# A row-sum kernel whose tile context is closed empty at the start, with all its work behind it on hand-made semaphores

## The chip, the cores and the metric

The kernel runs on one core of one Trainium2 chip. The metric is the device time of one execution in microseconds; the number given for a kernel is the median of its runs. Before the change it is 161.99 us (three runs, 161.81 to 162.04).

## What is computed

```python
def setup_inputs():
    batch, seq, dim = 32, 512, 1024
    return {"x": np.random.randn(batch, seq, dim).astype(np.float32), "multiplier": 0.5}

def reference(x, multiplier):
    return (np.sum(x, axis=-1) * multiplier).astype(np.float32)
```

16,384 rows of 1,024 floats each become one float each. The input is 67.1 MB, the output 64 KB.

## The kernel before

**Tiling.** Each of the 128 partitions owns 128 rows, taken as 8 blocks of 16 rows. A block is one tile `xb` of 128 x 16 x 1024 floats (8.4 MB), and three such buffers are used in turn. The first seven blocks are loaded by one transfer each (L98). The last block comes in five pieces: rows 0 to 7, 8 to 12 and 13 to 14 into the same kind of buffer (L117), and the last row in two parts, 544 and 480 floats, into a small tile `end` (L123). All transfers are issued by SP, on one queue.

**Compute.** VectorE (DVE) sums the 16 rows of a block with one `reduce_sum` into `sums` (L100) and scales them into `res` with a small instruction (L103). In the seventh block DVE takes only 8 rows; ScalarE (ACT) does the other 8, each by one `activation` with an accumulator (L74). ACT needs a table load ahead of its first activation. In the last block both share the rows: ACT the rows in `on_act`, DVE the others, by `tensor_tensor_reduce` (L84). The last row is two such instructions on `end`: `first` when its first part has landed, and `final`, which also folds in the result of `first`.

**Stores.** The results of the first seven blocks leave by an early store (L127, 56 KB), the last block's by the last store (L145, 8 KB). Both stand on SP's queue behind all loads.

**Order and waits.** The tile context works out the waits from the tiles: a load into a buffer waits until the DVE has read what lay in it, an instruction waits for its load, and so on. Where the kernel wants a wait in a place of its own, `nop_after` (L63) puts an empty instruction with that wait on an engine. The context also owns what stands at the end of the program: on its exit (L208 in the profile) SP waits for the last store, all five engines meet at a barrier, GpSimd (POOL) clears the range of semaphores that the context used, and all five meet at a second barrier. The program's entry (L194) has a barrier of the same build. `start_loads_at_entry` takes the leading loads of SP, those that wait for nothing (three, one for each buffer), and puts them ahead of SP's part in the entry barrier, so that the first transfer is SP's first instruction.

Of the kernel before, what the change touches and what calls it, by code (L numbers as in the profile page):

```python
# [1 line left out]

# [4 lines left out]


@with_exitstack
def kernel(  # L10
    ctx: ExitStack,
    tc: tile.TileContext,
    x: bass.AP,
    multiplier: float,
    out: bass.AP,
):

    nc = tc.nc
    P = nc.NUM_PARTITIONS
    fp32 = mybir.dt.float32  # L30
    ADD = mybir.AluOpType.add

    x_flat = x.flatten_outer_dims()
    N, D = x_flat.shape
    rows = N // P
    out_flat = out.rearrange("b s -> (b s)")
    mul = float(multiplier)

    B = 16
    n_blocks = rows // B  # L40
    assert N == P * rows and rows == n_blocks * B
    own = rows - B
    x_rows = x_flat[0 : P * own, :].rearrange("(p c) d -> p c d", p=P)
    x_last = x_flat[P * own : N, :].rearrange("(p c) d -> p c d", p=P)
    out_rows = out_flat[0 : P * own].rearrange("(p c) -> p c", p=P)
    out_last = out_flat[P * own : N].rearrange("(p c) -> p c", p=P)

    x_pool = ctx.enter_context(tc.tile_pool(name="x", bufs=3))
    res_pool = ctx.enter_context(tc.tile_pool(name="res", bufs=1))
    sums = res_pool.tile([P, rows], fp32, name="sums")  # L50
    res = res_pool.tile([P, rows], fp32, name="res")
    cut = 544
    at = 576
    end = res_pool.tile([P, at + D - cut], fp32, name="end")
    nc.vector.memset(end[:, at - 2 : at], 0.0)  # L55

    SYNC = mybir.DependencyInfo(mybir.DependencyClass.Sync, mybir.DependencyReason.DATA)
    ORDER = mybir.DependencyInfo(
        mybir.DependencyClass.NoSync, mybir.DependencyReason.SCHED_ONLY
    )  # L60

    def nop_after(engine, waits_for, follows):
        i = engine.nop()  # L63
        for w in waits_for:
            tc.add_manual_dep(i.ins, w.ins.name, SYNC, reason="end seen here")
        for f in follows:
            tc.add_manual_dep(i.ins, f.ins.name, ORDER, reason="in this order")
        return i

    loads = []  # L70
    acts = []

    def act_row(t, r, col):
        acts.append(nc.scalar.activation(  # L74
            out=t[:, r, :],
            in_=t[:, r, :],
            func=mybir.ActivationFunctionType.Copy,
            scale=mul,
            accum_out=res[:, col : col + 1],
        ))  # L80

    def dve_sum(row, dst, scale):
        mid = row.shape[-1] // 2
        return nc.vector.tensor_tensor_reduce(  # L84
            out=row[:, 0:mid],
            in0=row[:, 0:mid],
            in1=row[:, mid:],
            scale=scale,
            scalar=0.0,
            op0=ADD,  # L90
            op1=ADD,
            accum_out=dst,
        )

    for b in range(n_blocks - 1):
        c0 = b * B
        t = x_pool.tile([P, B, D], fp32, name="xb")
        loads.append(nc.sync.dma_start(out=t, in_=x_rows[:, c0 : c0 + B, :]))  # L98
        h = B if b < n_blocks - 2 else B // 2
        nc.vector.reduce_sum(  # L100
            out=sums[:, c0 : c0 + h], in_=t[:, 0:h, :], axis=mybir.AxisListType.X
        )
        nc.vector.tensor_single_scalar(  # L103
            out=res[:, c0 : c0 + h],
            in_=sums[:, c0 : c0 + h],
            scalar=mul,
            op=mybir.AluOpType.mult,
        )
        for r in range(h, B):
            act_row(t, r, c0 + r)  # L110

    c0 = (n_blocks - 1) * B
    t = x_pool.tile([P, B, D], fp32, name="xb")
    pieces = [(0, 8), (8, 13), (13, 15)]
    for lo, hi in pieces:
        loads.append(
            nc.sync.dma_start(  # L117
                out=t[:, lo:hi, :], in_=x_last[:, lo:hi, :]
            )
        )  # L120
    for to, lo, hi in ((0, 0, cut), (at, cut, D)):
        loads.append(
            nc.sync.dma_start(  # L123
                out=end[:, to : to + hi - lo], in_=x_last[:, B - 1, lo:hi]
            )
        )
    early = nc.sync.dma_start(out=out_rows, in_=res[:, 0:own])  # L127
    on_act = {4, 5, 6, 7, 11, 12, 14}
    for r in range(B - 1):
        if r in on_act:  # L130
            act_row(t, r, c0 + r)
        else:
            dve_sum(t[:, r, :], res[:, c0 + r : c0 + r + 1], mul)
    first = dve_sum(end[:, 0:cut], end[:, at - 1 : at], 1.0)
    part_seen = nop_after(nc.vector, [first], [])
    final = dve_sum(end[:, at - 2 :], res[:, rows - 1 : rows], mul)

    tc.add_manual_dep(final.ins, part_seen.ins.name, ORDER, reason="in this order")
    tc.declare_no_dep(final.ins, first.ins.name, reason="waited for by the nop in front")

    seen = nop_after(nc.sync, loads[-8:] + acts[-1:], [])
    store = nc.sync.dma_start(out=out_last, in_=res[:, own:])  # L145
    tc.add_manual_dep(store.ins, seen.ins.name, ORDER, reason="in this order")
    for a in acts[-len(on_act) :]:
        tc.declare_no_dep(store.ins, a.ins.name, reason="waited for by the nop in front")
    nop_after(nc.sync, [early, final], [store])

    def start_loads_at_entry(nc_):

        entry, *rest = nc_.main_func.blocks
        is_sp = lambda i: i.engine == mybir.EngineType.SP
        is_load = lambda i: type(i).__name__ == "InstDMACopy"
        for block in rest:
            body = list(block.instructions)
            own = [i for i in body if is_sp(i)]  # L160
            if not any(is_load(i) for i in own):
                continue
            lead = []
            for i in own:
                if not is_load(i) or i.sync_info.on_wait:
                    break
                lead.append(i)
            names = {i.name for i in lead}
            block.instructions = [i for i in body if i.name not in names]
            head = list(entry.instructions)  # L170
            at = next(
                k for k, i in enumerate(head) if is_sp(i) and type(i).__name__ == "InstDrain"
            )
            entry.instructions = head[:at] + lead + head[at:]
            return

    nc.at_finalize(start_loads_at_entry)


# [1 line left out]
_INS = ['x', 'multiplier']  # L181
_OUTS = [((32, 512), 'float32')]

_NUMBERS = {'multiplier': 0.5}


# [26 lines left out]
```

## The time and the profile before

| what | value |
|---|---|
| median of three runs | 161.99 us |
| span of the profiled execution, first to last instruction | 160.2 us |
| median less this span (the page gives the profiled execution no time of its own beside the span) | 1.79 us |
| DMA queue: bytes, share of 16 engines' span | 67.18 MB, 97.6% |
| DVE busy | 119.3 us (74%) |
| ACT busy | 17.3 us (11%) |
| POOL busy | 0.2 us |

The span counts from the first to the last instruction on any engine, waits and barriers included; the busy times leave out register, branch, semaphore and DMA-issuing instructions. SP does no arithmetic and shows only as `SPq`: its issues of transfers and its semaphore instructions. A transfer's time from issue to landing includes the time in which it stands behind others in the queue.

### The profile page before, as it was taken

The numbers are of one execution on the slowest core, as the hardware profiler recorded it, in microseconds if no ns is written. First come the engines' busy times: TensorE is split into PE (matmuls) and PEld (weight loads), VectorE is DVE, ScalarE is ACT, GpSimd is POOL, SyncE is SP. The second block draws the span as 40 slices with busy tenths as digits, with TensorE's granted clock in tenths as the row PEclk, the third lists the DMA queues.
The fourth block names the chain that finished last, engine by engine and source line by source line (L and its number), as shares of the span: only waits on it lengthen the run. The fifth ranks groups of instructions, "written<-read, shape, count | busy, mean of one in ns | idle before, by whom it ended". The sixth has DMA issues, their size and how long they took to land.

```text
span 160.2 us, 139 instructions
## 1 busy us (share of the span) xinstructions
DVE 119.3 (74%) x35; ACT 17.3 (11%) x31; POOL 0.2 (0%) x4
## 2 busy tenths in 40 slices
DVE  0000059998799968999599995999959999597543
ACT  0000000000000000000000000000000000599952
POOL 0000000000000000000000000000000000000000
DMA  8996996996996997997998989979969969999992
GB/s 278 507 524 262 524 524 262 524 524 262 524 507 278 524 475 311 524 442 344 524 425 360 524 360 425 524 327 458 524 295 491 524 278 507 393 401 422 424 395 76
DMA packets 2016, 67.18 MB, mean 419 GB/s; under 512 B 480, under 2 KB 608, under 8 KB 736
## 3 DMA queue, kind: packets, MB, share of 16 engines
q1 hardware_dynamic: 2016, 67.18, 97.6%
HBM read 67.11 MB, written 0.07 MB: 419 GB/s over the span
## 4 chain that ended last, share of the span: by engine, by line
DMA 75%; DVE 22%; SPq 1%; issue 0%; DVEq 0%
DMA xb<-in_x_dram 51%; DMA end<-in_x_dram 24%; DVE sums L100 22%; SPq L117 1%; SPq L123 0%; DVE end L84 0%; SPq L98 0%; DVE res L103 0%; DVEq L208 0%
## 5 line engine op out<-in xcount | busy, mean ns | idle before, releaser
L100 DVE TENSOR_REDUCE sums<-xb 128x16 f32<-128x16384 f32 (+1 forms) x7 | 112.0, 16002 | 31.5 <-DMA xb<-in_x_dram 31.5
L74 ACT ACT_TABLE_LOAD x1 | 1.3, 1283 | 138.0 <-DMA xb<-in_x_dram 138.0
L74 ACT ACTIVATE xb<-xb 128x1024 f32<-128x1024 f32 x15 | 15.7, 1044 | 2.1 <-DMA xb<-in_x_dram 2.1
L84 DVE CUSTOM_DVE_ANT_0 xb<-xb 128x512 f32<-128x512 f32 x8 | 5.1, 690 | 4.9 <-DMA xb<-in_x_dram 4.9
L74 ACT ACTIVATION_READ_ACCUMULATOR xb<-xb 128x1 f32 x15 | 2.8, 187 | 0.0
L55 DVE MEMSET end<- 128x2 f32 x1 | 0.1, 60 | 1.8 <-PEq L194 1.8
L103 DVE TENSOR_SCALAR res<-sums 128x16 f32<-128x16 f32 (+1 forms) x7 | 1.2, 174 | 0.2
L84 DVE CUSTOM_DVE_ANT_0 end<-end 128x272 f32<-128x272 f32 (+1 forms) x2 | 0.9, 426 | 0.2 <-DMA end<-in_x_dram 0.2
L84 DVE DVE_READ_ACCUMULATOR2_ANT res<- 128x1 f32 x9 | 0.7, 83 | 0.0
L194 POOL MEMSET const-bfloat16-1.0<- 128x1 bf16 x1 | 0.1, 102 | 0.0
L194 POOL MEMSET const-uint8-127<- 128x1 uint8 x1 | 0.1, 102 | 0.0
L194 POOL MEMSET const-float32-0.0<- 128x1 f32 x1 | 0.1, 99 | 0.2 <-issue 0.2
L194 POOL MEMSET const-float32-1.0<- 128x1 f32 x1 | 0.1, 99 | 0.0
L84 DVE DVE_READ_ACCUMULATOR2_ANT end<- 128x1 f32 x1 | 0.1, 83 | 0.0
## 6 DMA issues: line engine op xcount, KB each, us to landing
xb<-in_x_dram SPq DMA_DIRECT2D x1, 4096.0 KB, 31.1
xb<-in_x_dram SPq DMA_DIRECT2D x1, 2560.0 KB, 36.9
xb<-in_x_dram SPq DMA_DIRECT2D x1, 1024.0 KB, 38.9
end<-in_x_dram SPq DMA_DIRECT2D x1, 272.0 KB, 39.0
end<-in_x_dram SPq DMA_DIRECT2D x1, 240.0 KB, 39.2
xb<-in_x_dram SPq DMA_DIRECT2D x7, 40.8
out_dram<-res SPq DMA_DIRECT2D x1, 56.0 KB, 10.0
out_dram<-res SPq DMA_DIRECT2D x1, 8.0 KB, 1.4
```

Of the source, the lines that this page charges most:

```text
L55: nc.vector.memset(end[:, at - 2 : at], 0.0)
L74: acts.append(nc.scalar.activation(out=t[:, r, :], in_=t[:, r, :], func=mybir.ActivationFunctionType.Copy, scale=mul, accum_out=res[:, col ...
L84: return nc.vector.tensor_tensor_reduce(out=row[:, 0:mid], in0=row[:, 0:mid], in1=row[:, mid:], scale=scale, scalar=0.0, op0=ADD, op1=ADD, ...
L100: nc.vector.reduce_sum(out=sums[:, c0 : c0 + h], in_=t[:, 0:h, :], axis=mybir.AxisListType.X)
L103: nc.vector.tensor_single_scalar(out=res[:, c0 : c0 + h], in_=sums[:, c0 : c0 + h], scalar=mul, op=mybir.AluOpType.mult,)
L117: nc.sync.dma_start(out=t[:, lo:hi, :], in_=x_last[:, lo:hi, :])
L194: nc = _bacc.Bacc("TRN2", target_bir_lowering=False, num_devices=1)
```

## The change

The tile context is closed and compiled as soon as the kernel function starts, with nothing in it. What it puts at its end (two barriers, with no semaphores to clear) therefore stands right behind the program's entry, and a new body of the program begins after it. Everything else is written with plain SBUF tensors and semaphores by hand: one semaphore for each load, one counting DVE's instructions and one counting ACT's. The loads, the arithmetic, the split between the engines, the sizes and `start_loads_at_entry` are as before. At its end SP waits for the two stores, and the program ends there.

```diff
     nc = tc.nc
+    tc.close()
+    tc.compile()
+    nc.switch_body("work")
...
+    def load(name, dst, src, free=None):
+        landed = sem(name)
+        i = nc.sync.dma_start(out=dst, in_=src)
+        if free is not None:
+            i.wait_op(dve_done, free, "sem-ge")
+        i.then_inc(landed, 16)
+        return landed
...
-        loads.append(nc.sync.dma_start(out=t, in_=x_rows[:, c0 : c0 + B, :]))
+        t = buf[b % bufs]
+        landed = load(
+            f"landed{b}",
+            t,
+            x_rows[:, c0 : c0 + B, :],
+            freed[b - bufs] if b >= bufs else None,
+        )
...
+        if h < B:
+            nc.scalar.wait_ge(landed, 16)
+            for r in range(h, B):
+                i = act_row(t, r, c0 + r)
+            early_act = marks(i, "act")
...
+    nc.sync.wait_ge(dve_done, early_dve)
     early = nc.sync.dma_start(out=out_rows, in_=res[:, 0:own])
+    early.wait_op(act_done, early_act, "sem-ge")
...
-    part_seen = nop_after(nc.vector, [first], [])
+    part = marks(first, "dve")
+    nc.vector.wait_ge(dve_done, part)
     final = dve_sum(end[:, at - 2 :], res[:, rows - 1 : rows], mul)
+    final.wait_op(landed_end[1], 16, "sem-ge")
+    done = marks(final, "dve")
...
-    seen = nop_after(nc.sync, loads[-8:] + acts[-1:], [])
+    nc.sync.wait_ge(act_done, late_act)
     store = nc.sync.dma_start(out=out_last, in_=res[:, own:])
-    nop_after(nc.sync, [early, final], [store])
+    store.wait_op(dve_done, done, "sem-ge")
+    stored = sem("stored")
+    store.then_inc(stored, 16)
+    nc.sync.wait_ge(early_stored, 16)
+    nc.sync.wait_ge(stored, 16)
```

In the order of the built program the three leading loads are still SP's first instructions, ahead of the entry barrier. Two things in it are not in the diff's words: the ACT table load now stands directly behind the barriers, with no wait on a load in front of it, and the second and third `xb` buffers have exchanged their addresses.

## The prediction

> **What bounds the kernel now.** I read the page's totals first, then the timeline, then the records of the context's closing line (L208), then SP's own waits. From the page:
>
> ```profile
> span 160.2 us, 139 instructions
> ...
> DVE 119.3 (74%) x35; ACT 17.3 (11%) x31; POOL 0.2 (0%) x4
> ...
> q1 hardware_dynamic: 2016, 67.18, 97.6%
> ```
>
> The DMA queue is busy for 97.6% of the span and DVE for 74%, so the input stream sets the pace. The timeline (start us, duration us, what, and in brackets the idle time before it) shows how closely:
>
> ```profile
> 0.00 97.51 SPq L98 DMA_DIRECT2D xb<-in_x_dram  x7
> ...
> 1.81 0.06 DVE L55 MEMSET end<- 128x2 f32 x1 [1.81 <-PEq L194]
> 21.91 17.22 DVE L100 TENSOR_REDUCE sums<-xb 128x16 f32<-128x16384 f32 x1 [20.04 <-DMA xb<-in_x_dram]
> ...
> 41.23 17.22 DVE L100 TENSOR_REDUCE sums<-xb 128x16 f32<-128x16384 f32 x1 [1.89 <-DMA xb<-in_x_dram]
> ...
> 138.05 1.28 ACT L74 ACT_TABLE_LOAD   x1 [138.05 <-DMA xb<-in_x_dram]
> ...
> 157.58 0.41 DVE L84 CUSTOM_DVE_ANT_0 end<-end 128x241 f32<-128x241 f32 x1 [0.16 <-DMA end<-in_x_dram]
> 157.91 0.08 DVE L84 DVE_READ_ACCUMULATOR2_ANT res<- 128x1 f32 x1
> 158.02 0.34 SPq L145 DMA_DIRECT2D out_dram<-res  x1
> ```
>
> Every reduction starts when its load lands. The last piece of input lands just before 157.58, DVE works 0.41 us on it, the last store is issued at 158.02, and the page's sixth part gives it 1.4 us to landing: 159.4. The span ends at 160.2. The chain of waits stops at DVE's closing drain at 157.99 and so leaves out this tail; it is in the records of L208 (duration least/median/most in ns, then first and last start in us):
>
> ```profile
> L208 POOLq EVENT_SEMAPHORE  x4: 17/17/17, 159.6 to 160.1; - x4
> ...
> L208 SPq DRAIN  x3: 7/7/7, 159.5 to 159.8; - x3
> ...
> L208 PEldq EVENT_SEMAPHORE  x2: 51/51/51, 159.7 to 160.2; - x2
> ...
> L208 POOLq EVENT_SEMAPHORE_RANGE_CLEAR  x1: 93/93/93, 159.8 to 159.8; - x1
> ```
>
> The first SP drain is where the last store is seen; its record starts at 159.468. The last record, TensorE's release from the second barrier, starts at 160.153 and takes 0.051: 160.204. The stretch between is one barrier (released at about 159.7), the clearing of semaphores, and a second barrier: 160.204 - 159.468 = 0.74 us in which nothing of the problem is done and nothing else runs.
>
> **The change part by part, on the profiled execution (span 160.20).** The runs' median lies 1.79 us above this span. The page shows no time of the profiled execution itself, so I carry 1.79 over as a constant; whether it is one is a rival below.
>
> *The tail.* What stands behind the last store's landing goes: 0.74 us. In its place SP has one semaphore instruction that waits for both stores; SP's two-wait instructions ahead of L145 last 0.028 us. The early store has landed by then (issued at 147.79, 10.0 us to landing, 157.8). Net 0.74 - 0.03 = **-0.71 us**. No other engine works there, so all of it is on the path.
>
> *The head.* The two barriers now run behind the entry barrier, which ends at about 1.7 us. At the tail the two rounds took 0.74 us, the clear included, so the engines come free at about 2.4 instead of 1.7. DVE's memset (1.81) moves to about 2.5; its first reduction waits until 21.91, 19 us of cover. SP's first three loads stand ahead of all barriers in the built program's order, so the stream still starts at 0.00. SP's fourth load waits for the first reduction's end at 39.1, 36 us later. Cost 0. If the cover were gone, as it would be were the loads behind the barriers, the whole stream would start about 2.4 us later.
>
> *The ACT table load.* It no longer waits for a load and moves from 138.05 into the idle 2.4 to 21.9. ACT's first activation then starts at about 138.05 instead of 139.34, and its eight rows end at about 146.5 instead of 147.8. What is late next: the first piece of the last block, which lands at 147.7, and the second, whose rows start at 153.79. ACT is caught by these loads again, so nothing reaches the end: 0.
>
> *The early store.* SP holds it for ACT:
>
> ```profile
> SPq L127 <- DVE res L103: 28.0, 1, 28.0
> ...
> SPq L208 <- DMA out_dram<-res: 1.0, 1, 1.0
> ...
> SPq L127 <- ACT xb L74: 0.9, 1, 0.9
> ```
>
> That wait of 0.9 us goes; DVE's scaling at 146.70 + 0.17 is late next, so it is issued at about 146.95 instead of 147.79. All loads were issued by 118.9, and the store stayed behind them (10.0 us to landing) until the last input had landed at 157.55. I take 0. If its packets do get in between, they push the last load back by at most 56 KB at the page's mean 419 GB/s = 0.13 us; an earlier store could instead take up to the same from what stands behind the loads. Bounds -0.13 to +0.13.
>
> *Waits by hand.* Each reduction, activation and load waits for the same event as before. SP loses its second wait ahead of the buffered loads (17 ns each, long over when DVE ends) and four of the waiting instructions ahead of the last store. These end by 157.76, and DVE's last result comes at 157.99, so SP waits there anyhow: 0. DVE keeps its one wait between `first` and `final` (0.021 us at 157.45, before the last part lands at 157.55). Behind SP's new wait for ACT stands only the last store, and ACT's last row ended at 157.44, before DVE's. At most the order of SP's waking changes; from rows of 0.02 to 0.03 us I bound it by -0.03 to +0.03.
>
> *Buffers.* The second and third buffer exchange addresses. In the timeline the reductions start at 21.91, 41.23, 60.58, 79.94, 99.28, 118.63 and 137.98, so spacings are 19.32 to 19.36 whichever buffer is filled and whichever is read. I take 0; both ends are 0.04 us for each of seven loads, -0.28 to +0.28. The value taken is the one nearest to these rows, which show no dependence.
>
> Sum: 160.20 - 0.71 = 159.49 for the span, and 161.99 - 0.71 = **161.28 us** for the time (-0.44%). A measurement of this kernel can tell about 0.2%, 0.32 us, from no change; -0.71 is more than twice that.
>
> **A rule beside the rows.** Nothing in the trace shows the 1.79 us around the span. The Trainium skill, "Runtime: NRT & Kernel Launch", section "The ~15µs preamble/postamble breakdown", says that the runtime puts its own barrier of about 1.5 us behind every kernel and then resets 51 semaphores on each engine in about 1.5 us. That speaks against the change in one way: a meeting of the engines is still paid after the kernel's barriers are gone. But by that rule it was paid before as well, and on a fixed count of semaphores, so the estimate by the page is again -0.71. By its stages of 1.5 + 1.5 + 2 us after the kernel, more than 1.79 us, they cannot all be inside the measured time; no row settles which are.
>
> **The rivals.**
>
> *The outside shrinks too.* TensorE and POOL now end at about 2.4 us and only SP is late at the end. If part of the 1.79 us is work that each engine does for itself after its last instruction, four engines do it under the cover of the kernel. The nearest row is the second barrier with its clear, 159.77 to 160.20 = 0.43 us. That gives 161.28 - 0.43 = 160.85. For it: all five engines end within 0.1 us today. Against it: SP, still last, does its own part uncovered.
>
> *The outside grows by what was cut.* If the measured end is a meeting that takes its full time from when the last engine arrives, and it had been running alongside the kernel's own barriers, the cut of 0.71 is given back: 161.99, no change. For it: nothing in the trace shows the measured end. Against: all engines left the last barrier at 160.15 to 160.20, so such a meeting could hardly begin before.
>
> *The leftover semaphores are cleared elsewhere: slower.* Before, POOL clears the context's ten in one 0.093 us instruction. After, sixteen hand-made ones are left standing. If what follows the kernel clears them one by one, at the 0.078 us between two successive POOL semaphore instructions of the barrier, this costs 16 x 0.078 = 1.25 us after the span: 161.28 + 1.25 = 162.53. It decides from 1.03 us on (0.71 + 0.32), 0.065 us each. At the bare 0.017 us of such an instruction it is 0.27 and the kernel stays faster. Against it: a clear of a range took 0.093.
>
> *The change doesn't do what it says.* If nobody clears them, every wait of a second execution is already met. DVE would run its 119.3 us without waiting and the program would end near 1.8 + 119.3 + 1.8 = 123 us, with sums of what an earlier execution left. The two barriers in the head clear nothing, so this can't be excluded from the trace.
>
> **How the numbers follow.** The forecast, with its small bounds (-0.13, -0.03, -0.28 on one side, the same on the other, partly together: 160.95 to 161.6), has 0.70. The outside shrinking (160.85) 0.12; giving back (161.99) 0.10; cleared one by one (162.53) 0.05; uncleared (123) 0.03. Faster by over 0.2%: 0.70 + 0.12 + 0.03 = 0.85; within: 0.10; slower: 0.05. The range runs from below 160.85, at 160.75, to 161.65, and leaves out 0.18.
>
> **What would show it.** In the changed profile SP's last record waits for the stores and ends near 159.5, with no barrier records behind it. Two barrier rounds stand between 1.7 and 2.5 us. The table load stands there too. The first reduction starts at 21.9, the spacings stay 19.3, the early store is issued near 146.95, and `final` starts near 157.58. I am wrong if the first load no longer starts the span, if the spacings move by 0.1 us, or if the span falls by 0.7 and the runs' time doesn't.

## The result, and the profile after the change

The changed kernel takes **160.73 us** (median of five runs, 160.69 to 160.89); the kernel before took 161.84 beside it (161.79 to 162.04, five runs, three of them those already told). The ratio is 0.9929, 95% interval 0.9917 to 0.9941: about 1.15 us faster. The forecast was 161.28 with a range of 160.75 to 161.65: the sign was right, the gain was under-estimated by 0.4 to 0.5 us, and the time lies 0.02 us under the range.

The page of the changed kernel:

```profile
span 159.4 us, 123 instructions
...
DVE 119.3 (75%) x35; ACT 17.3 (11%) x31; POOL 0.2 (0%) x4
...
q1 hardware_dynamic: 2016, 67.18, 98.0%
```

The work is the same; the span fell from 160.2 to 159.4. The timeline (start us, duration us, what, idle before):

```profile
2.39 1.28 ACT L82 ACT_TABLE_LOAD   x1 [2.39 <-PEq L26]
2.46 0.06 DVE L103 MEMSET end<- 128x2 f32 x1 [2.46 <-PEq L26]
21.84 17.22 DVE L117 TENSOR_REDUCE sums<-xb 128x16 f32<-128x16384 f32 x1 [19.31 <-DMA xb<-in_x_dram]
...
41.18 17.22 DVE L117 TENSOR_REDUCE sums<-xb 128x16 f32<-128x16384 f32 x1 [1.91 <-DMA xb<-in_x_dram]
...
157.51 0.41 DVE L92 CUSTOM_DVE_ANT_0 end<-end 128x241 f32<-128x241 f32 x1 [0.15 <-DMA end<-in_x_dram]
157.85 0.08 DVE L92 DVE_READ_ACCUMULATOR2_ANT res<- 128x1 f32 x1
157.96 0.34 SPq L175 DMA_DIRECT2D out_dram<-res  x1
```

The stream starts and runs as before, within 0.07 us at every reduction and at `final`. The closing barriers are in the head, at the line that compiles the empty context (L26; durations in ns, then first and last start in us), and after the last store only SP's wait is left (L180, a view of its own):

```profile
L26 POOLq EVENT_SEMAPHORE  x4: 17/17/17, 1.9 to 2.3; - x4
...
L26 PEldq EVENT_SEMAPHORE  x2: 51/51/51, 2.0 to 2.3; - x2
```

```profile
L180 SPq EVENT_SEMAPHORE  x1: 28/28/28, 159.4 to 159.4; - x1
```

All of this is as forecast. What was not: the profiled run's own time is 160.73, so the time above the span is 160.73 - 159.42 = 1.31 us. In the runs of before beside the experiments, time less span (given to 0.1 us) is 1.73 to 1.83 in each. The constant of 1.79 is no constant; it lost 0.48 us, and that is the part of the gain that the sum lacked.

### The profile page after: what moved, and what is told of

Read it like the earlier page. It is cut to its first block, busy times and chain, and to the rows that moved or that the text cites. A ratio compares the mean times of both kernels' runs of the same rounds, so it can differ in the third digit from the quotient of the medians.

```text
span 159.4 us, 123 instructions
## 1 busy us (share of the span) xinstructions
DVE 119.3 (75%) x35; ACT 17.3 (11%) x31; POOL 0.2 (0%) x4
## 4 chain that ended last, share of the span: by engine, by line
DMA 76%; DVE 22%; SPq 1%; issue 0%
DMA xb<-in_x_dram 51%; DMA end<-in_x_dram 25%; DVE sums L117 22%; SPq L75 1%; DVE end L92 0%; DVE res L123 0%; DVE res L92 0%
## 6 DMA issues: line engine op xcount, KB each, us to landing
out_dram<-res SPq DMA_DIRECT2D x1, 56.0 KB, 10.8
```

## The experiments

**Theory 1**: something of each engine's own follows its last instruction inside the measured time (its "own end" below), the engines do it side by side, and the time is the latest of last record + own end. The change leaves four engines' ends under the cover of the kernel. **Theory 2**: the time around the span became shorter for another reason, such as fewer branches, a shorter program or the missing clear. Each experiment was run beside runs of the kernel before, and its ratio is to those; the time above the span is taken run by run, and the median is given. A record is one instruction in the profile; its views round starts to 0.1 us, and the ends given to 0.01 us below are read from the same records.

The kernel before took 161.93 to 161.99 us (medians) beside the experiments, and 161.84 beside the result. So differences of medians between two experiments are good to about 0.1 us only, and several medians lie 0.01 to 0.07 us above the range that was written down for their outcome: all engines (161.28) and GpSimd alone (161.32, both for at most 161.25), the barrier of four (161.42 for 161.39), the head alone (162.02 for 161.99), the left semaphores and the late table (160.81 and 160.83 for 160.80).

### All engines wait for the last store

```diff
     nc.sync.wait_ge(early_stored, 16)
     nc.sync.wait_ge(stored, 16)
+    nc.tensor.wait_ge(stored, 16)
+    nc.gpsimd.wait_ge(stored, 16)
+    nc.scalar.wait_ge(stored, 16)
+    nc.vector.wait_ge(stored, 16)
```

> The changed kernel with four waits added: TensorE, GpSimd, ScalarE and VectorE also wait for the last store, so all five engines end together, with no barrier. The span can grow by 0.05 us at most (one semaphore instruction of 0.02 to 0.05 us side by side on each). Theory 1 (each engine has something of its own to do after its last instruction, inside the measured time; the change lets four engines do it under cover): the time above the span returns from 1.31 to 1.64-1.79 us, so the time is 161.05 to 161.25. Theory 2 (the time around the span became shorter for another reason: fewer branches, fewer instructions, no clear of semaphores at the end): the time above the span stays 1.31, the time is 160.73 to 160.80.

Measured: 161.28 us (161.23 to 161.31), ratio 0.9957 (0.9944 to 0.9971). The last record of each engine, each from the view of its own line:

```profile
L180 SPq EVENT_SEMAPHORE  x1: 28/28/28, 159.4 to 159.4; - x1
...
L181 PEldq EVENT_SEMAPHORE  x1: 51/51/51, 159.4 to 159.4; - x1
...
L182 POOLq EVENT_SEMAPHORE  x1: 17/17/17, 159.4 to 159.4; - x1
...
L183 ACTq EVENT_SEMAPHORE  x1: 17/17/17, 159.4 to 159.4; - x1
...
L184 DVEq EVENT_SEMAPHORE  x1: 21/21/21, 159.4 to 159.4; - x1
```

All five engines end between 159.43 and 159.47, with a span of 159.5, and the time above it is 1.81 us, near that of the kernel before. There is no barrier, no clear, no branch more than in the changed kernel. Theory 2 falls: which engines end late decides, and that alone gives back 0.45 us of the gain by the ratios, 0.55 by the medians.

### One engine at a time

The same edit with the TensorE line alone:

```diff
+    nc.tensor.wait_ge(stored, 16)
```

> The changed kernel with one wait added: TensorE alone also waits for the last store. Theory 1, with TensorE the engine whose end costs most: 161.05 to 161.25, as with all engines; theory 1 with another engine the costly one: 160.73 to 160.80. Theory 2: 160.73 to 160.80.

Measured: 161.10 us (161.02 to 161.24), ratio 0.9947 (0.9935 to 0.996). And with the GpSimd line alone:

```diff
+    nc.gpsimd.wait_ge(stored, 16)
```

> The changed kernel with one wait added: GpSimd alone also waits for the last store. Theory 1, with GpSimd the engine whose end costs most: 161.05 to 161.25; with another engine the costly one: 160.73 to 160.80. Theory 2: 160.73 to 160.80.

Measured: 161.32 us (161.24 to 161.52), ratio 0.9961 (0.9948 to 0.9973): as much as all four together, so the ends do not add up; the longest counts. TensorE's time lies in the range written down for the engine whose end costs most, but that range was set too low: TensorE's end costs too, but less than GpSimd's. The profiled run of the GpSimd kernel took 161.52, with this one added record (its L181):

```profile
L181 POOLq EVENT_SEMAPHORE  x1: 17/17/17, 159.7 to 159.7; - x1
```

It ends with SP's last record (159.67 and 159.68), and yet this run's time lies 161.52 - 159.67 = 1.85 above it instead of 1.31. With the same 1.85, GpSimd's end at 159.44 in the run of all engines gives 161.29; that run took 161.28.

### GpSimd waits, but ends sooner

```diff
+    nc.gpsimd.wait_ge(dve_done, done)
```

> The changed kernel with one wait added: GpSimd also waits, but for VectorE's last result (about 157.93) instead of the last store's landing (159.4). Theory 1, the time being the latest of (last record + own end) over the engines: GpSimd at 157.97 + 1.85 = 159.82 is under SP's 159.42 + 1.31 = 160.73, so the time is that of the changed kernel, 160.70 to 160.85. Rival (any late wait on GpSimd costs, as a longer program or a busy semaphore does): 161.0 to 161.3, as with its wait for the store.

Measured: 160.74 us (160.67 to 160.96), ratio 0.9925 (0.9913 to 0.9938): no cost. The same kind of wait on the same engine, for another semaphore and 1.4 us ahead of SP's last record:

```profile
L181 POOLq EVENT_SEMAPHORE  x1: 17/17/17, 158.0 to 158.0; - x1
```

158.0 + 1.85 = 159.8 is under SP's 160.73. So it is not a late instruction on GpSimd as such that costs but where the engine's end falls, as theory 1 says.

### The last wait on another engine

ScalarE in SP's place, then VectorE:

```diff
-    nc.sync.wait_ge(early_stored, 16)
-    nc.sync.wait_ge(stored, 16)
+    nc.scalar.wait_ge(early_stored, 16)
+    nc.scalar.wait_ge(stored, 16)
```

> The changed kernel with the last wait moved: ScalarE instead of SP waits for the two stores, and SP ends when it has issued the last store. Theory 1 with a cost of its own for each engine: the time moves by the difference between ScalarE's end and SP's, so not above 161.25 and below 160.73 if ScalarE's is the shorter. Theory 2: 160.73, the span being the same.

Measured: 161.10 us (160.88 to 161.14), ratio 0.9943 (0.9931 to 0.9956), time above the span 1.48. With `nc.vector` in the two added lines instead:

> The changed kernel with the last wait moved: VectorE instead of SP waits for the two stores. Theory 1: the time is the last record (159.4) plus VectorE's own end, which no run so far shows. From the four known ends (1.31 to 1.85) it is 160.7 to 161.25; below 160.68 it would be a version better than the changed kernel. Rival (ends are all alike and the waits of the other runs cost something else): 160.73.

Measured: 160.92 us (160.83 to 161.02), ratio 0.9934 (0.9922 to 0.9947), time above the span 1.42. Neither beats SP. For VectorE the ratio alone can't tell it from the changed kernel's; the time above the span can, at 1.42 to 1.43 in every run against 1.29 to 1.33. The own ends, as profiled run's time less the end of the engine's last record:

| engine that ends last | from | own end, us |
|---|---|---|
| SP | 160.73 - 159.42 | 1.31 |
| VectorE | 161.02 - 159.61 | 1.41 |
| ScalarE | 160.88 - 159.39 | 1.49 |
| TensorE | 161.16 - 159.53 | 1.63 |
| GpSimd | 161.52 - 159.67 | 1.85 |

The records of the three engines not yet shown, each from a run and a view of its own (TensorE with its wait, then ScalarE and VectorE in SP's place):

```profile
L181 PEldq EVENT_SEMAPHORE  x1: 51/51/51, 159.5 to 159.5; - x1
...
L180 ACTq EVENT_SEMAPHORE  x1: 38/38/38, 159.4 to 159.4; - x1
...
L180 DVEq EVENT_SEMAPHORE  x1: 50/50/50, 159.6 to 159.6; - x1
```

SP's figure comes out at 1.31 again in four more profiled runs (the earlier end of GpSimd, the left semaphores, the loads behind, the late table), and GpSimd's at 1.84 to 1.87 in three (all engines, the barrier of five, the head alone). The figures of VectorE and ScalarE rest on one profiled run each. What stands ahead of SP's first instruction is inside each figure and is taken to be the same in all; the runs don't divide the two.

### One barrier back at the end

```diff
     nc.sync.wait_ge(early_stored, 16)
     nc.sync.wait_ge(stored, 16)
+    nc.all_engine_barrier()
```

> The changed kernel with one barrier of all engines put back at the very end, behind SP's wait for the stores; no clear of semaphores. In the profile of before one such round took 0.22 us from SP's drain to the release, GpSimd's last record in it ending some 0.09 us ahead of the others'. The span grows to about 159.7. Theory 1 with the ends measured so far (time above the engine's own last record: SP 1.31, TensorE 1.63, ScalarE 1.5, GpSimd 1.85): GpSimd at 159.61 + 1.85 = 161.46, TensorE at 159.70 + 1.63 = 161.33, so 161.40 to 161.55. Rival (only the barrier's own length counts, the time above the span stays 1.31): 161.0.

Measured: 161.48 us (161.40 to 161.60), ratio 0.9971 (0.9959 to 0.9982). Its records at the end (L181 there):

```profile
L181 POOLq EVENT_SEMAPHORE  x2: 17/17/17, 159.6 to 159.7; - x2
...
L181 SPq DRAIN  x1: 7/7/7, 159.6 to 159.6; - x1
...
L181 PEldq EVENT_SEMAPHORE  x1: 51/51/51, 159.8 to 159.8; - x1
```

In the profiled run (161.60) GpSimd's last record ends at 159.73, and 159.73 + 1.85 = 161.58. TensorE's, last in the span, ends at 159.82 and would give 161.45 only. A single round of 0.25 us from SP's wait to the last release thus costs about 0.7 us of time (0.68 by the ratios, 0.75 by the medians), because it brings GpSimd's longer end to the finish.

### A barrier without GpSimd

```diff
+    nc.multi_engine_barrier([nc.sync.engine, nc.scalar.engine, nc.vector.engine, nc.tensor.engine])
```

> The changed kernel with one barrier at the very end, of SP, ScalarE, VectorE and TensorE, led by ScalarE, without GpSimd. Theory 1: TensorE is released last, at about 159.70 to 159.75, and has the longest own end of the four: + 1.64 = 161.34 to 161.39; SP's, at 159.72 + 1.31 = 161.03, is under it. Rival (a barrier at the end costs the same whoever is in it): 161.48, as with all five. Rival (only the length of the barrier counts): 161.0.

Measured: 161.42 us (161.37 to 161.62), ratio 0.9966 (0.9952 to 0.9979). By the medians this can't be told from the barrier of five. By the time above the span it can: 1.67 here, 1.78 there, as TensorE takes GpSimd's place:

```profile
L181 PEldq EVENT_SEMAPHORE  x1: 51/51/51, 159.8 to 159.8; - x1
```

This record ends at 159.84, and + 1.63 that is 161.47, against 161.50 for the profiled run. The release was expected at 159.70 to 159.75, so the forecast was low by that. The time excludes the rival that only the barrier's length counts (161.0); against the rival that a barrier costs the same whoever is in it (161.48) speaks only the time above the span.

### Semaphores left standing

```diff
+    for k in range(64):
+        nc.tensor.nop().then_inc(sem(f"left{k}"), 1)
```

> The changed kernel with 64 more semaphores, each raised once by TensorE in its idle time at the start and left standing at the end. If what follows the kernel clears a fixed number whatever was used: 160.73 to 160.80. If standing semaphores are cleared one by one inside the measured time, at 0.017 to 0.078 us each: 161.8 to 165.7.

Measured: 160.81 us (160.69 to 160.96), ratio 0.9927 (0.9915 to 0.9939), time above the span 1.31. Sixty-four more semaphores cost nothing that can be seen. Whether something clears them, and whether it does so under the cover of a longer end, this doesn't show.

### The head: two empty barriers alone, and the loads behind them

The kernel before, with an empty context ahead of its own:

```diff
+    with _tile.TileContext(nc):
+        pass
     with _tile.TileContext(nc) as tc:
         tile_sum_mul_kernel(tc, *args)
```

> The kernel before with an empty tile context opened and closed ahead of it: two more barriers behind the entry, the tail as before. By the prediction the head costs nothing (19 us of cover): the time of before, 161.85 to 161.99, the fourth load and the first reduction at the same moments. Rival (the extra barriers or branches delay the stream or the fetch of instructions): later by the 0.65 us of two rounds, 162.5.

Measured: 162.02 us (161.83 to 162.33), ratio 1.0004 (0.9995 to 1.0013): the head costs nothing. Then the changed kernel with the loads left behind the barriers:

```diff
-    nc.at_finalize(start_loads_at_entry)
```

> The changed kernel without the step that puts the first three loads ahead of the entry barrier, so that SP issues its first load behind the entry barrier and the two empty ones. The prediction said that the stream would then start 2.4 us later: 163.1. Its rival from the changed profile: SP's drain is then no longer held back by three issues of 0.43 us, the entry barrier is over at about 0.7 and each further round takes 0.33, so the stream starts 1.3 to 1.4 us later: 162.0 to 162.2, and the gain of the change is gone.

Measured: 162.18 us (162.05 to 162.36), ratio 1.0011 (1.0002 to 1.002): the whole gain is gone. Its timeline:

```profile
1.38 1.33 SPq L75 DMA_DIRECT2D xb<-in_x_dram  x3
1.39 1.28 ACT L82 ACT_TABLE_LOAD   x1 [1.39 <-PEq L26]
1.46 0.06 DVE L103 MEMSET end<- 128x2 f32 x1 [1.46 <-PEq L26]
23.27 17.22 DVE L117 TENSOR_REDUCE sums<-xb 128x16 f32<-128x16384 f32 x1 [21.75 <-DMA xb<-in_x_dram]
```

The stream starts 1.38 us late and the first reduction 1.43. With no loads to issue ahead of SP's drain, the entry barrier is over at 0.7 us instead of 1.7; the 2.4 us of the prediction had kept these issues in the sum.

### The table load late, as before

```diff
             for r in range(h, B):
                 i = act_row(t, r, c0 + r)
+                if r == h:
+                    i.wait_op(dve_done, freed[3], "sem-ge")
```

The added wait is long met; with it, ScalarE waits for the load in an instruction of its own, which in the profile stands ahead of the table load (it ends at 138.04).

> The changed kernel with the ACT table load held back until the seventh block has landed, as before: ScalarE's first activation starts at about 139.2 instead of 137.93, and the early store is issued at about 147.7 instead of 146.91. By the prediction this costs nothing: 160.73 to 160.80. Rival (the earlier table load or the earlier early store is part of the gain): 160.85 to 161.1.

Measured: 160.83 us (160.66 to 161.05), ratio 0.9928 (0.9916 to 0.9941), the changed kernel's. The table load and the early store stand where they stood before the change:

```profile
138.08 1.28 ACT L82 ACT_TABLE_LOAD   x1 [138.08 <-DMA xb<-in_x_dram]
...
147.82 0.35 SPq L152 DMA_DIRECT2D out_dram<-res  x1
```

Neither is part of the gain.

## Why the prediction was wrong, step by step

*The tail.* Right. The span lost 0.74 us from drain to release and got SP's 0.028 back. It went from 160.204 to 159.416, 0.08 more than that, because SP saw the last store 0.08 us sooner in this execution (159.388 against 159.468); its last part of the input had come 0.07 sooner.

*The constant around the span.* This is the step that failed: "so I carry 1.79 over as a constant". It was 1.31 afterwards. The cause is shown by adding one wait: the same changed kernel has 1.31 above its span when SP alone ends last and 1.84 when GpSimd ends with it. In the kernel before, GpSimd leads the closing barriers, and its last record ends at 160.116; + 1.85 = 161.97. The runs of before with this span, 160.2, took 161.93 to 162.03. In the kernel with the empty context ahead of it, which has the same closing barriers, the same figure can be measured: 161.83 - 159.97 = 1.86. In the changed kernel SP ends at 159.416; + 1.31 = 160.73. Between the two ends lie 160.116 - 159.416 = 0.70 us; 0.08 of it is the store that was seen sooner, and 0.62 is the barriers. With 1.85 - 1.31 = 0.54 of GpSimd's longer end this makes 1.16, against 1.15 by the ratio. Counted by the span, which before ends 0.09 us behind GpSimd with TensorE's record, the same gain reads 0.71 of barriers and 0.45 to 0.48 of the time above the span.

*The rival "the outside shrinks too".* This was the mechanism, and it had 0.12. It was priced at 0.43 from the second barrier, for want of a row, and measured 0.48. The argument against it, that SP does its own part uncovered, was true but weaker than thought, since SP's part is the shortest of the five. With all engines ending within 0.1 us before the change, the longest own end would set the time if the ends differed at all; the rival deserved more weight.

*The other rivals.* "Given back" (161.99) falls with the result. The price of "cleared one by one" falls with 64 more semaphores at no cost. This is in keeping with what the Trainium skill says in "Runtime: NRT & Kernel Launch", section "The ~15µs preamble/postamble breakdown", that 51 semaphores on each engine are reset after a kernel; no run here shows that reset itself. "Nobody clears them" (123 us) falls with 160.73.

*The page's rule.* The same section puts a barrier of all engines behind every kernel. The prediction concluded that this is paid before and after alike, so that the sum stays at -0.71. Measured in the profiled runs, a last arrival only 0.06 us later (159.47 for 159.42) gives a time 0.55 us longer (161.28 for 160.73) when GpSimd is among the late ones, so what follows the kernel isn't a fixed time from the last arrival. Which of the page's stages lie in the measured time no run here shows.

*The head.* Right at 0. Its price without the cover was wrong: 1.4 us, not 2.4, so the forecast that the loads behind the barriers start the stream 2.4 us later was too high by 1.0.

*The table load and the early store.* Right at 0: ScalarE was caught by the loads again, and the store, issued at 146.91 as forecast (146.95), took 10.8 us to land instead of 10.0. SP's waits ahead of it and after it:

```profile
SPq L149 <- DVE res L123: 28.1, 1, 28.1
...
SPq L180 <- DMA out_dram<-res: 1.1, 1, 1.1
```

Ahead of the early store the wait for ScalarE is gone, as expected, and the last one is for the store alone.

*Waits by hand and exchanged buffers.* Right at 0: the reductions start 19.34 to 19.36 us apart (19.32 to 19.36 before).

What stays open is what happens in an engine's own end, why GpSimd's is the longest, and how much of each figure stands ahead of the first instruction. It need not be work of the engine itself: if the engines were gathered one after another behind the kernel, each engine's place in that order would give the same rule, the latest of last record + a figure of the engine. No run here tells the two apart.

## What to carry to other kernels

Closing barriers cost more than their own length when they bring the engine with the longest own end to the finish; ask not only when the last instruction ends but which engine it is on. An engine with nothing to do at the end should be let go early, and the last wait be put on the engine whose end is the shortest, SP in these runs. A time carried over from outside the span is a term of the sum like any other, with bounds of its own, and a step that holds the stream's start (here 1.4 us) must stay ahead of whatever is moved into the head.

## What the runs showed that was not expected

The time above an engine's last record depends on the engine: 1.31 us on SP, 1.41 on VectorE, 1.49 on ScalarE, 1.63 on TensorE, 1.85 on GpSimd. The ends run side by side: GpSimd alone at the end (161.32) costs as much as all five (161.28), and nothing when it ends 1.4 us ahead of SP (160.74). One barrier of all engines, 0.25 us long, cost about 0.7 us at the end of the program, and two cost nothing at its start with the first loads ahead of them (ratio 1.0004).
